# An accumulating DMA that makes the low parts of the input projection's weights in a hybrid decoder layer

## The chip, the cores and the metric

The kernel runs on one core of a Trainium2 chip. The metric is the device time of one execution in microseconds (us); lower is better. The engines are PE (TensorE: matmuls, PEld its weight loads), DVE (VectorE), ACT (ScalarE), POOL (GpSimd) and SP (SyncE, which issues most of the DMAs).

## What is computed

One decoder layer, batch 1, 1024 tokens, 1024 channels, all in float32. The part that the change touches is the product `proj = u @ w_in[l]`:

```
u = _rmsnorm(h, norm_g[l]) * (1.0 + scale) + shift
proj = u @ w_in[l]                       # [1024, 1024] x [1024, 7168]
a = conv_a * jax.nn.sigmoid(conv_bp)     # convolution branch: 31 taps, layer norm, pointwise, gate
q, k, v, ret_gate                        # retention branch: 4 heads of 256, rotary, group norm, gate
y = jnp.concatenate([y_conv, y_ret], axis=-1) @ w_out[l]
h = h + gate * y                         # then a final rms norm
```

## The kernel before

PE multiplies in a format (`F32R`) that keeps fewer bits than float32. So each operand is split into a high part (a cast to `F32R`) and a low part (the operand minus its high part), and each product is three matmuls that add up in PSUM: high by high (L71), high by low of the activations (L72), low of the weights by high (L73). This is `mm3`.

A **unit** is 128 columns of `w_in`: eight steps over the input channels, two halves of 512 tokens, three matmuls each, 48 matmuls in all. While the modulated input u is built (the head of the program), four units run along with it from weights loaded by another function. The other 44 of this kind go through `in_unit` (L246) and are counted here as units 0 to 43 in the order in which PE takes them; the eight column blocks of v are done elsewhere (`values`, L329, which calls `load_w` itself).

For each unit `load_w` (L61) does four things. SP loads the 512 KB of weights into a tile `raw` (L63). ACT casts them into `hi` (`split`, L58). DVE subtracts, `lo = raw - hi` (L59). PE then reads `hi` and `lo`. The tiles `raw`, `hi` and `lo` have two buffers each, shared with the weights of v and with those of the later projections. So the cast of unit n can only start when unit n-2 has made its last matmul on `hi`, and its matmuls on `lo` can only start when DVE is done.

The instructions of each engine run in the order that the tile framework's scheduler gives them when the kernel is built. The convolution's taps (L239, 240 instructions on DVE, in `conv_taps`) have a low priority and fill whatever time DVE has left. A unit's sums leave PSUM by ACT or DVE, at the end of the unit: by copies for the rotary embedding (L315), by sigmoid or silu activations (L254, L465, L267), or by DVE products. The retention's own matmuls are put between those of the units. POOL has little to do: a power of -0.5 for the norms (L422) and clearing the 30 columns of padding ahead of each convolution input `a` (L256), which waits until the taps have finished with that buffer, of which there are two.

After the last unit come the two halves of the output projection, the layer norm of the convolution branch and the pointwise convolution. They use `load_w` too, and the change leaves them as they are.

Of the kernel before, what the change touches and what calls it, by code (L numbers as in the profile page):

```python
# [7 lines left out]
F32 = mybir.dt.float32  # L8
F32R = mybir.dt.float32r
# [3 lines left out]
P = 128  # L13
# [3 lines left out]
KT = D // P  # L17
# [5 lines left out]
CH = 256  # L23
NCH = S // CH
HALF = 512
EARLY = (8, 0, 9, 1)  # the units that run while u is built

# columns of the packed per-channel vectors
V_C, V_SH, V_SC, V_NG, V_CB, V_LG, V_LB, V_GG, V_GB, V_CW = 0, 8, 16, 24, 32, 40, 48, 56, 64, 72
V_N = V_CW + KT * CW  # L30
# columns of the packed decay constants
K_G, K_G2, K_KD = 0, 2 * H, 4 * H
K_N = 6 * H

# [4 lines left out]
def hybrid_layer(ctx: ExitStack, tc: tile.TileContext, x, vec, c_row, ada_ss, ada_g, adab_g, w_e, w_m, w_v,  # L39
                 w_pw, w_out, final_g, cs, masks, kc, ident, out):  # L40
    nc = tc.nc
    SUB, ADD, MUL = ALU.subtract, ALU.add, ALU.mult
# [10 lines left out]
    d_yc = dram.tile([4, P, S], F32, name="d_yc")  # L53
    d_h1 = dram.tile([TT, P, D], F32, name="d_h1")

# [1 line left out]
    def split(hi, lo, src):  # L57
        nc.scalar.copy(hi, src)  # L58
        nc.vector.tensor_tensor(lo, src, hi.bitcast(F32), op=SUB)  # L59
# [1 line left out]
    def load_w(src, shape, name, pool=None):  # L61
        raw = wpool.tile(shape, F32, tag="raw", name=f"raw_{name}")
        nc.sync.dma_start(raw, src)  # L63
        pool = pool or wpool
        hi = pool.tile(shape, F32R, tag="hi", name=f"hi_{name}", bufs=2)
        lo = pool.tile(shape, F32R, tag="lo", name=f"lo_{name}", bufs=2)
        split(hi, lo, raw)
        return hi, lo

    def mm3(ps, lh, ll, rh, rl, start, stop):  # L70
        nc.tensor.matmul(ps, lh, rh, start=start, stop=False)  # L71
        nc.tensor.matmul(ps, lh, rl, start=False, stop=False)  # L72
        nc.tensor.matmul(ps, ll, rh, start=False, stop=stop)  # L73

    def unit(wh, wl, rh, rl, name, halves_first=False, pool=None, tag="mm"):
        """[128 columns of w]^T times the resident operand, both halves of its free axis."""
        ps = [(pool or mmp).tile([P, HALF], F32, tag=tag, name=f"ps_{name}_{i}") for i in range(2)]
        order = [(k, i) for k in range(KT) for i in range(2)]
        if halves_first:
            order.sort(key=lambda o: o[1])  # L80
        for k, i in order:
            sl = slice(i * HALF, (i + 1) * HALF)
            mm3(ps[i], wh[:, k], wl[:, k], rh[k][:, sl], rl[k][:, sl], k == 0, k == KT - 1)
        return ps

# [1 line left out]
    vec_t = const.tile([P, V_N], F32, name="vec_t")  # L87
    ident_t = const.tile([P, P], F32, name="ident_t")
    kc_t = const.tile([P, K_N], F32, name="kc_t")
# [10 lines left out]
        return vec_t[:, base + k:base + k + 1]  # L100

    def bcast_rsqrt(pool, psp, sums, scale, n, rb):
        """sums: [128, n] column sums (token t = 128 j + partition); rb: PSUM [128, 128 n] gets rsqrt in every row."""
        v = pool.tile([P, n], F32, tag="rs_v", name="rs_v")
        nc.vector.tensor_scalar(v, sums, scale, EPS, op0=MUL, op1=ADD)
        r = pool.tile([P, n], F32, tag="rs_r", name="rs_r")
        nc.gpsimd.tensor_tensor(r, v, mhalf[:, :n], op=ALU.pow)
        for j in range(n):
            dg = pool.tile([P, P], F32, tag="rs_d", name="rs_d", bufs=4)
            nc.vector.tensor_scalar(dg, ident_t, r[:, j:j + 1], None, op0=MUL)  # L110
            nc.tensor.matmul(rb[:, j * P:(j + 1) * P], ones_t, dg, start=True, stop=True)

# [1 line left out]
    xts = [big.tile([P, D], F32, tag="big", name=f"xt{t}", bufs=17) for t in range(TT)]  # L114
    uh = [big.tile([P, S], F32R, tag="big", name=f"uh{k}", bufs=17) for k in range(KT)]
    ul = [big.tile([P, S], F32R, tag="big", name=f"ul{k}", bufs=17) for k in range(KT)]
# [6 lines left out]
    hps = head_ctx.enter_context(tc.tile_pool(name="headps", bufs=1, space=bass.MemoryType.PSUM))  # L123

    def head():
        """Builds u tile by tile and runs the first four units along with it, k on the outside."""
        xs = hp.tile([P, KT, S], F32, name="xs")
        cbc = hp.tile([P, D], F32, name="cbc")
        junk2 = hp.tile([P, D], mybir.dt.bfloat16, name="junk2")
# [21 lines left out]
            nc.sync.dma_start(xts[t], x[t])  # L151

        def norm(t, xt_):
            """x / rms(x) of 128 tokens, turned so that features are on partitions."""
            ms = hp.tile([P, 1], F32, tag="ms", name=f"ms{t}", bufs=3)
            nc.scalar.activation(junk2, xt_, AF.Square, scale=D ** -0.5, accum_out=ms)
            nc.gpsimd.tensor_scalar(ms, ms, EPS, None, op0=ADD)
            nc.gpsimd.tensor_tensor(ms, ms, mhalf[:, 0:1], op=ALU.pow)
            nc.vector.tensor_scalar(xt_, xt_, ms, None, op0=MUL)
            for q in range(2):  # L160
                tp = hps.tile([P, 4, P], F32, tag=("paa", "pbb", "pcc", "pdd")[(2 * t + q) % 4], name=f"xp{t}{q}")
                for j in range(4):
                    k = 4 * q + j
                    nc.tensor.transpose(tp[:, j], xt_[:, k * P:(k + 1) * P], ident_t)
                dst = xs[:, 4 * q:4 * q + 4, t * P:(t + 1) * P]
                if q == 0 and t < 7:
                    nc.scalar.copy(dst, tp)
                else:
                    nc.vector.tensor_copy(dst, tp)
# [61 lines left out]
        return ps  # L231

    def conv_taps(m, ap):
        """Convolves one tile of channels; fills whatever time the vector engine has left."""
        with tc.high_priority(offset=-TAPS_LATER):
            y = convp.tile([P, S], F32, tag="y", name=f"y{m}")
            nc.vector.tensor_scalar(y, ap[:, 0:S], col(V_CW, m * CW), col(V_CB, m), op0=MUL, op1=ADD)
            for j in range(1, CW):
                nc.vector.scalar_tensor_tensor(y, ap[:, j:j + S], col(V_CW, m * CW + j), y, op0=MUL, op1=ADD)  # L239
            nc.sync.dma_start(d_y[m], y)  # L240
            if m == 0:
                nc.vector.tensor_copy(ysum, y)
            else:
                nc.vector.tensor_tensor(ysum, ysum, y, op=ADD)

    def in_unit(n):  # L246
        wh, wl = load_w(w_m[n - sum(e < n for e in EARLY)], [P, KT, P], f"w{n}")
        return unit(wh, wl, uh, ul, f"w{n}")

    def conv_pair(m, early=None):  # L250
# [25 lines left out]
    gate_steps = []  # L276

    def out_gate():
        """One step towards the residual's gate, the same in every partition."""
        k = len(gate_steps)  # L280
        if k == 0:
            gate_steps.append(const.tile([P, D], F32, name="gacc"))
        else:
            gate_steps.append(None)
        acc = gate_steps[0]
        if k < KT:
            raw = wpool.tile([P, D], F32, tag="raw", name=f"ag{k}")
            nc.sync.dma_start(raw, ada_g[k])
            if k == 0:
                nc.vector.tensor_scalar(acc, raw, cact[:, 0:1], None, op0=MUL)  # L290
            else:
                nc.vector.scalar_tensor_tensor(acc, raw, cact[:, k:k + 1], acc, op0=MUL, op1=ADD)
            return
        agb = wpool.tile([P, D], F32, tag="raw", name="agb")
        nc.sync.dma_start(agb, adab_g.broadcast_to([P, D]))
        for i in range(2):
            sl = slice(i * HALF, (i + 1) * HALF)
            gp = mmp.tile([P, HALF], F32, tag="mm", name=f"gp{i}")
            nc.tensor.matmul(gp, ones_t, acc[:, sl], start=True, stop=True)
            nc.vector.tensor_tensor(acc[:, sl], gp, agb[:, sl], op=ADD)  # L300

# [1 line left out]
    with tc.tile_pool(name="ret", bufs=1, reuse_waits="tile") as rp, \  # L303
            tc.tile_pool(name="retps", bufs=1, space=bass.MemoryType.PSUM) as rps:

# [38 lines left out]
        def retention(h, q, k, v, sg):  # L344
            state = st_h = st_l = None
            for c in range(NCH):
                ts = slice(c * CH, (c + 1) * CH)
                n = f"{h}{c}"
# [6 lines left out]

                vh, vl = chunk("vc", v[:, 2 * c:2 * c + 2])
                if c < NCH - 1:
                    # keys with tokens on partitions, decayed to the chunk's end
                    kth = rp.tile([P, 2, 2 * P], F32R, tag="kth", name=f"kth{n}")
                    ktl = rp.tile([P, 2, 2 * P], F32R, tag="ktl", name=f"ktl{n}")  # L360
                    for j in range(2):
# [8 lines left out]
                kh, kl = chunk("kc", k[:, :, ts])  # L370
                qh, ql = chunk("qc", q[:, :, ts])

                # scores, transposed: keys on partitions
                sp = rps.tile([P, 3 * P], F32, tag="sp", name=f"sp{n}")
                for d in range(2):
                    mm3(sp[:, 0:CH], kh[:, d, 0:P], kl[:, d, 0:P], qh[:, d], ql[:, d], d == 0, d == 1)
# [6 lines left out]
                sl_ = rp.tile([P, 3 * P], F32R, tag="sl", name=f"sl{n}", bufs=1)  # L383
                split(sh, sl_, sm)

                # outputs, tokens on partitions
                op = rps.tile([P, 2, 2 * P], F32, tag="op", name=f"op{n}")
                mm3(op[:, 0], sh[:, 0:P], sl_[:, 0:P], vh[:, 0], vl[:, 0], True, False)
                mm3(op[:, 1], sh[:, P:CH], sl_[:, P:CH], vh[:, 0], vl[:, 0], False, False)
# [19 lines left out]
                    st_l = rp.tile([P, 2, 2 * P], F32R, tag="stl", name=f"stl{n}")  # L409
                    split(st_h, st_l, state)  # L410

                # group norm over the head's 256 values
                st6 = rp.tile([P, 2, 6], F32, tag="st6", name=f"st6{n}", bufs=2)
                mv = rp.tile([P, 2, 2], F32, tag="mv", name=f"mv{n}", bufs=2)
                for i in range(2):
# [58 lines left out]
        f2 = ctx.enter_context(tc.tile_pool(name="fin2", bufs=1, reuse_waits="tile", side="right"))  # L474
        y3 = f2.tile([P, 3, S], F32, tag="y3", name="y3")
        negmu = f2.tile([P, S], F32, tag="y1", name="negmu")
        # layer norm, channels on partitions; what fits in before u is gone comes first
        def ln_center(m, tmp):
            if m < 3:
                yt = y3[:, m]  # L480
# [18 lines left out]
        for m in range(2, KT):  # L499
            conv_gate(m)  # L500

# [1 line left out]
    with tc.tile_pool(name="fin", bufs=1, reuse_waits="tile") as fp, \  # L503
            tc.tile_pool(name="finps", bufs=1, space=bass.MemoryType.PSUM) as fps:
        gate = gate_steps[0]
# [58 lines left out]
        fgt = fp.tile([P, D], F32, name="fgt")  # L564
        nc.sync.dma_start(fgt, final_g.broadcast_to([P, D]))

# [1 line left out]
        for m in range(KT):  # L568
            wh, wl = load_w(w_pw[m], [P, KT, P], f"pw{m}")
            ps = unit(wh, wl, zh, zl, f"pw{m}", m == KT - 1)  # L570
# [10 lines left out]
                nc.sync.dma_start(d_yc[m], cg)  # L581
            load_r(m, wpool, "raw")

# [1 line left out]
        for t in range(TT):  # L585
            hi = wpool.tile([P, KT, P], F32R, tag="hi", name=f"ych{t}")
            lo = wpool.tile([P, KT, P], F32R, tag="lo", name=f"ycl{t}")
# [46 lines left out]
def _layout(inp):  # L634
# [25 lines left out]
    ada_ss = c(ada_w[:, :2 * D].reshape(D, 2, KT, P).transpose(2, 3, 1, 0))  # L660
    ada_ss[0, :, 0] = ada_w[:, :P].reshape(KT, P, P).transpose(1, 0, 2).reshape(P, D)

    # tables that depend on the shapes alone
    f4 = np.float32
    inv = (f4(1.0) / np.power(f4(10000.0), np.linspace(0.0, 1.0, P, dtype=f4))).astype(f4)
    theta = (np.arange(S, dtype=f4)[None, :] * inv[:, None]).astype(np.float64)
# [50 lines left out]
```

## Time and profile before

| | us |
|---|---|
| median of 2 runs (1003.21 to 1003.64) | 1003.42 |
| the profiled execution, from its first to its last instruction | 1001.6 |
| of these, PE busy | 987.8 |
| DVE busy | 739.3 |
| ACT busy | 312.8 |
| POOL busy | 35.9 |

The profile is one execution on the chip. The time of a run takes in what lies around the span: the median is 1.8 us above the span of the profiled execution. The ends of matmuls are modelled, so PE's busy time is not its peak rate.

### The profile page before, as it was taken

What the parts mean: (1) busy time and instruction counts of PE and PEld (TensorE: products, weight loads), DVE (VectorE), ACT (ScalarE), POOL (GpSimd) and SP (SyncE); (2) the same over time, 40 slices, a digit from 0 to 9 for tenths busy, and PEclk for the clock granted to TensorE, in tenths of its full rate; (3) what the DMA queues carried; (4) which work ended last, traced back from release to release, by engine and by line L of the source; (5) the groups of instructions that cost most, each with busy time, mean ns of one, the idle gap of its engine ahead of it and who ended that gap; (6) DMA issues with size and microseconds to landing.
All of it is one profiled execution on the core that took longest, in us unless ns stands there. A gap on an engine that the chain in (4) does not pass through costs nothing.

```text
span 1001.6 us, 12564 instructions
## 1 busy us (share of the span) xinstructions
PE 987.8 (99%) x5108; PEld 843.6 (84%) x5108; DVE 739.3 (74%) x969; ACT 312.8 (31%) x489; POOL 35.9 (4%) x55
## 2 busy tenths in 40 slices
PE   7999999999999999999999999999999999999997
PEld 5888899888898888899888898888888888888886
DVE  6959999899998999999967679764446963442342
ACT  7831223332213322223233412443422711111221
POOL 2000000000000000100000000000000000000000
PEclk9999999999999999999999999999999999999999
DMA  9641111111132211113221022411784356541322
GB/s 351 236 168 43 43 43 64 63 64 43 64 106 74 74 63 63 43 64 127 63 84 42 25 103 63 147 64 64 264 277 152 127 172 209 187 137 63 127 95 84
DMA packets 40253, 108.80 MB, mean 109 GB/s; under 512 B 3458, under 2 KB 16002, under 8 KB 39043
## 3 DMA queue, kind: packets, MB, share of 16 engines
q1 hardware_dynamic: 40050, 107.74, 31.5%
q8 instruction: 40, 0.66, 0.3%
q10 hardware_dynamic: 144, 0.26, 0.1%
q14 instruction: 19, 0.15, 0.0%
HBM read 84.92 MB, written 23.07 MB: 108 GB/s over the span
## 4 chain that ended last, share of the span: by engine, by line
PE 96%; DVE 1%; DMA 1%; ACT 0%; issue 0%; SPq 0%; POOL 0%; POOLq 0%; DVEq 0%; ACTq 0%
PE ps_w L73 16%; PE ps_w L71 16%; PE ps_w L72 16%; PE ps_v L71 3%; PE ps_v L73 3%; PE ps_v L72 3%; PE ps_oc L73 3%; PE ps_or L72 3%; PE ps_oc L72 3%; PE ps_oc L71 3%; PE ps_or L73 3%; PE ps_pw L73 3%; PE ps_pw L71 3%; PE ps_or L71 3%; PE ps_pw L72 3%; PE op L73 1%
## 5 line engine op out<-in xcount | busy, mean ns | idle before, releaser
L239 DVE SCALAR_TENSOR_TENSOR y<-a,vec_t,y 128x1024 f32<-128x1024 f32 x240 | 300.5, 1278 | 1.3
L72 PE MATMUL ps_w<-ul,hi_w 128*128 128x512 f32 x704 | 275.2, 391 | 0.0
L73 PE MATMUL ps_w<-uh,lo_w 128*128 128x512 f32 x704 | 274.8, 391 | 0.0
L71 PE MATMUL ps_w<-uh,hi_w 128*128 128x512 f32 x704 | 274.6, 391 | 0.0
L72 PEld LDWEIGHTS ps_w<-ul,hi_w 128*128 128x128 f32 x704 | 132.3, 188 | 26.2 <-issue 0.2
L71 PEld LDWEIGHTS ps_w<-uh,hi_w 128*128 128x128 f32 x704 | 132.3, 188 | 25.9 <-issue 0.2
L73 PEld LDWEIGHTS ps_w<-uh,lo_w 128*128 128x128 f32 x704 | 132.2, 188 | 25.7
L72 PE MATMUL ps_v<-lo_v,uh 128*128 128x256 f32 x256 | 72.1, 283 | 0.0
L73 PE MATMUL ps_v<-hi_v,ul 128*128 128x256 f32 x256 | 71.8, 283 | 0.0
L71 PE MATMUL ps_v<-hi_v,uh 128*128 128x256 f32 x256 | 71.7, 283 | 0.0
L59 DVE TENSOR_TENSOR lo_w<-raw_w,hi_w 128x1024 fp32r<-128x1024 f32 x44 | 53.7, 1220 | 23.2 <-ACT hi_w L58 23.1
L58 ACT CAST hi_w<-raw_w 128x1024 fp32r<-128x1024 f32 x44 | 46.2, 1049 | 69.8 <-PE ps_w L72 27.5
L72 PE MATMUL ps_oc<-wol,ych 128*128 128x512 f32 (+1 forms) x136 | 51.2, 377 | 0.0
L73 PE MATMUL ps_oc<-woh,ycl 128*128 128x512 f32 (+1 forms) x136 | 51.2, 376 | 0.0
L71 PE MATMUL ps_oc<-woh,ych 128*128 128x512 f32 (+1 forms) x136 | 51.2, 376 | 0.0
L71 PE MATMUL ps_pw<-zh,hi_pw 128*128 128x512 f32 x128 | 49.8, 389 | 0.0
L72 PE MATMUL ps_pw<-zl,hi_pw 128*128 128x512 f32 x128 | 49.8, 389 | 0.0
L73 PE MATMUL ps_pw<-zh,lo_pw 128*128 128x512 f32 x128 | 49.8, 389 | 0.0
L72 PE MATMUL ps_or<-wol,hi_yr 128*128 128x512 f32 x128 | 49.8, 390 | 0.0
L73 PE MATMUL ps_or<-woh,lo_yr 128*128 128x512 f32 x128 | 49.6, 390 | 0.0
L71 PE MATMUL ps_or<-woh,hi_yr 128*128 128x512 f32 x128 | 49.4, 390 | 0.0
L72 PEld LDWEIGHTS ps_v<-lo_v,uh 128*128 128x128 f32 x256 | 49.0, 192 | 0.2
(219 smaller groups left out, 1552.4 us busy)
## 6 DMA issues: line engine op xcount, KB each, us to landing
raw_w<-w_m SPq DMA_DIRECT2D x44, 512.0 KB, 3.5
xt<-x SPq DMA_DIRECT2D x16, 512.0 KB, 4.5
aw<-ada_ss SPq DMA_DIRECT2D x8, 1024.0 KB, 6.7
wo<-w_out SPq DMA_DIRECT2D x16, 512.0 KB, 5.4
raw_v<-w_v SPq DMA_DIRECT2D x8, 512.0 KB, 3.5
d_y<-y SPq DMA_DIRECT2D x8, 512.0 KB, 2.9
ag<-ada_g SPq DMA_DIRECT2D x8, 512.0 KB, 3.5
d_yr<-sg SPq DMA_DIRECT2D x8, 512.0 KB, 2.8
```

The lines of the kernel that those rows point to most:

```text
L58: nc.scalar.copy(hi, src)
L59: nc.vector.tensor_tensor(lo, src, hi.bitcast(F32), op=SUB)
L71: nc.tensor.matmul(ps, lh, rh, start=start, stop=False)
L72: nc.tensor.matmul(ps, lh, rl, start=False, stop=False)
L73: nc.tensor.matmul(ps, ll, rh, start=False, stop=stop)
L239: nc.vector.scalar_tensor_tensor(y, ap[:, j:j + S], col(V_CW, m * CW + j), y, op0=MUL, op1=ADD)
```

## The change

A new function, `load_wa`, takes the place of `load_w` in `in_unit`, and nowhere else. The raw load and the cast stay. ACT then writes the negated high part into `lo` (`lo = -hi`), and a DMA issued by POOL reads the same weights from memory a second time and adds them to `lo`, which makes `raw - hi`. DVE's subtraction of these 44 units is gone. Removed comments and docstrings are left out of the diff.

```
+    def load_wa(src, shape, name):
+
+        raw = wpool.tile(shape, F32, tag="raw", name=f"raw_{name}")
+        nc.sync.dma_start(raw, src)
+        hi = wpool.tile(shape, F32R, tag="hi", name=f"hi_{name}", bufs=2)
+        lo = wpool.tile(shape, F32R, tag="lo", name=f"lo_{name}", bufs=2)
+        nc.scalar.copy(hi, raw)
+        nc.scalar.mul(lo, hi.bitcast(F32), -1.0)
+        nc.gpsimd.dma_start(lo, src, accum_op=ADD)
+        return hi, lo
...
     def in_unit(n):
-        wh, wl = load_w(w_m[n - sum(e < n for e in EARLY)], [P, KT, P], f"w{n}")
+        wh, wl = load_wa(w_m[n - sum(e < n for e in EARLY)], [P, KT, P], f"w{n}")
         return unit(wh, wl, uh, ul, f"w{n}")
```

The scheduler also orders all engines anew. In the changed kernel the cast of these units is L76, the negation L77 and the DMA L78; what stood from L70 on in the kernel before is 11 lines further down (L71 to L73 are L82 to L84).

ACT at the first three units of `in_unit`: `hi_w_717`, `hi_w_775` and `hi_w_845` before are the high parts of units 0, 1 and 2; `sig` is the sigmoid of units that ran in the head, `x_q` the copy of unit 0's sums. Before:

```order
L58 CAST hi_w_717<-raw_w_715 128x1024
L254 ACT_TABLE_LOAD
L254 ACTIVATE sig_621<-ps_e_308 128x512
L254 ACTIVATE sig_621<-ps_e_309 128x512
L254 ACTIVATE sig_662<-ps_pcc 128x512
L254 ACTIVATE sig_662<-ps_pbb 128x512
L58 CAST hi_w_777<-raw_w_775 128x1024
L315 COPY x_q_713<-ps_w_0_721 128x512
L58 CAST hi_w_847<-raw_w_845 128x1024
L315 COPY x_q_713<-ps_w_1_722 128x512
```

ACT at the same place now (`hi_w_717`, `hi_w_778`, `hi_w_849`; `lo_w` are the negated parts):

```order
L76 CAST hi_w_717<-raw_w_715 128x1024
L265 ACT_TABLE_LOAD
L265 ACTIVATE sig_621<-ps_e_308 128x512
L77 ACTIVATE lo_w_718<-hi_w_717 128x1024
L265 ACTIVATE sig_621<-ps_e_309 128x512
L265 ACTIVATE sig_662<-ps_pcc 128x512
L265 ACTIVATE sig_662<-ps_pbb 128x512
L76 CAST hi_w_778<-raw_w_776 128x1024
L77 ACTIVATE lo_w_779<-hi_w_778 128x1024
L326 COPY x_q_713<-ps_w_0_722 128x512
L76 CAST hi_w_849<-raw_w_847 128x1024
L326 COPY x_q_713<-ps_w_1_723 128x512
```

Unit 0's negation stands behind a table load and the first sigmoid, unit 1's right behind its cast, and unit 2's behind a cast and the second copy of unit 0's sums.

PE at the first matmuls of unit 16, the first after the second head's v (`hi_w_2652` and `lo_w_2653` are its parts; `kp` and `sp` are transposes and scores of the retention). Before, from the unit's third matmul on:

```order
L71 MATMUL ps_w_1_2657<-uh_93,hi_w_2652 128x512
L72 MATMUL ps_w_1_2657<-ul_101,hi_w_2652 128x512
L364 MATMUL kp_2772<-ident_t,k_2151 128x128 x2
L71 MATMUL sp_2790<-qch_2786,kch_2782 128x256
L72 MATMUL sp_2790<-qcl_2787,kch_2782 128x256
L73 MATMUL ps_w_0_2656<-uh_93,lo_w_2653 128x512
L73 MATMUL ps_w_1_2657<-uh_93,lo_w_2653 128x512
```

PE now, from the third matmul of the scores on to the unit's first matmuls on its low part (`lo_w_2669`):

```order
L84 MATMUL sp_2808<-qch_2804,kcl_2801 128x256
L82 MATMUL sp_2808<-qch_2804,kch_2800 128x256
L83 MATMUL sp_2808<-qcl_2805,kch_2800 128x256
L84 MATMUL sp_2808<-qch_2804,kcl_2801 128x256
L82 MATMUL sp_2808<-qch_2804,kch_2800 128x128
L83 MATMUL sp_2808<-qcl_2805,kch_2800 128x128
L84 MATMUL sp_2808<-qch_2804,kcl_2801 128x128
L82 MATMUL sp_2808<-qch_2804,kch_2800 128x128
L83 MATMUL sp_2808<-qcl_2805,kch_2800 128x128
L84 MATMUL sp_2808<-qch_2804,kcl_2801 128x128
L84 MATMUL ps_w_0_2673<-uh_93,lo_w_2669 128x512
L84 MATMUL ps_w_1_2674<-uh_93,lo_w_2669 128x512
```

The ten other matmuls of the scores now stand ahead of the unit's first use of `lo`. The same stands at units 26 and 35, the first after the v of heads 3 and 4.

POOL around the padding of the fifth convolution input, before (`a_2339`) and then now (`a_2354`; `lo_w_2298` is the low part of unit 14):

```order
L422 TENSOR_TENSOR rs_1647<-rs_1647,mhalf 128x2
L422 TENSOR_TENSOR rs_1758<-rs_1758,mhalf 128x2
L422 TENSOR_TENSOR rs_1839<-rs_1839,mhalf 128x2
L256 MEMSET a_2339 128x30
L256 MEMSET a_3233 128x30
```

```order
L78 DMA lo_w_2167<-w_m 128x1024
L433 TENSOR_TENSOR rs_1766<-rs_1766,mhalf 128x2
L78 DMA lo_w_2228<-w_m 128x1024
L267 MEMSET a_2354 128x30
L78 DMA lo_w_2298<-w_m 128x1024
L433 TENSOR_TENSOR rs_1847<-rs_1847,mhalf 128x2
```

The DMAs of units 12 to 14 now stand between the norms' powers and the clearing of the padding, and unit 14's stands behind that clearing. What it waits for is the last tap on the third convolution input (`a_1034` before, `a_1039` now). DVE around the instruction that follows those taps (`ysum`), before and then now:

```order
L292 SCALAR_TENSOR_TENSOR gacc<-ag_2646,cact,gacc 128x1024
L260 TENSOR_TENSOR a_2339<-ps_w_0_2347,sig_2280 128x512
L244 TENSOR_TENSOR ysum<-ysum,y_1094 128x1024
L260 TENSOR_TENSOR a_2339<-ps_w_1_2348,sig_2280 128x512
L239 SCALAR_TENSOR_TENSOR y_1982<-a_1922,vec_t,y_1982 128x1024
L59 TENSOR_TENSOR lo_v_2443<-raw_v_2440,hi_v_2442 128x1024
```

```order
L333 TENSOR_TENSOR rb_q_2146<-ps_w_0_2096,cs_t 128x512
L335 TENSOR_TENSOR rd_q_2148<-ps_w_0_2096,cs_t 128x512
L250 SCALAR_TENSOR_TENSOR y_1100<-a_1039,vec_t,y_1100 128x1024
L250 SCALAR_TENSOR_TENSOR y_1992<-a_1931,vec_t,y_1992 128x1024
L336 TENSOR_TENSOR q_2027<-q_2027,rb_q_2146 128x512
L337 TENSOR_TENSOR q_2027<-q_2027,rd_q_2148 128x512
L255 TENSOR_TENSOR ysum<-ysum,y_1100 128x1024
```

Before, the taps end beside the product that makes the fifth input (`a_2339`); now they end beside the rotary products of unit 11 (`rb_q_2146`), four units earlier.

## Rows read from the trace of the kernel before

**Rows 1.** Page of the kernel before, part 2: the span in 40 slices, tenths.
```profile
PE   7999999999999999999999999999999999999997
...
PEclk9999999999999999999999999999999999999999
```

**Rows 2.** Windows: length, busy (count) of PE, PEld, DVE, ACT, POOL; clock, DMA share, GB/s.
```profile
0.00:68.00 68.00, 60.58 (x278) 48.37 (x279) 48.99 (x75) 48.49 (x75) 7.41 (x22) 1.00 0.73 270
68.00:730.00 662.00, 662.00 (x3625) 574.33 (x3624) 560.03 (x714) 196.14 (x310) 21.91 (x22) 1.00 0.23 77
```

**Rows 3.** Groups of instructions: busy us, mean ns of one, idle before.
```profile
L59 DVE TENSOR_TENSOR lo_w<-raw_w,hi_w 128x1024 fp32r<-128x1024 f32 x44 | 53.7, 1220 | 23.2 <-ACT hi_w L58 23.1
...
L58 ACT CAST hi_w<-raw_w 128x1024 fp32r<-128x1024 f32 x44 | 46.2, 1049 | 69.8 <-PE ps_w L72 27.5 <-issue 23.7 <-PE ps_v L73 13.7
...
L237 DVE TENSOR_SCALAR y<-a,vec_t 128x1024 f32<-128x1024 f32 x8 | 6.4, 806 | 0.1
...
L489 ACT ACTIVATE sq<-yt 128x1024 f32<-128x1024 f32 x5 | 5.2, 1058 | 10.9 <-DMA d_h<-xt 7.4 <-DVE ysum L490 3.5
```

**Rows 4.** Timeline of ACT, 60 to 102 us: start, length, instruction.
```profile
62.17 1.05 ACT L58 CAST hi_w<-raw_w 128x1024 fp32r<-128x1024 f32 x1 [4.82 <-PE ps_pdd L72]
63.24 1.28 ACT L254 ACT_TABLE_LOAD   x1
64.54 1.09 ACT L254 ACTIVATE sig<-ps_e 128x512 f32<-128x512 f32 x2
...
78.52 1.05 ACT L58 CAST hi_w<-raw_w 128x1024 fp32r<-128x1024 f32 x1
79.48 0.58 ACT L315 COPY x_q<-ps_w 128x512 f32<-128x512 f32 x1
```

**Rows 5.** Timeline of PE at the first use of units 0 and 2.
```profile
68.55 0.62 PE L73 MATMUL ps_w<-uh,lo_w 128*128 128x512 f32 x2
...
89.40 0.39 PE L71 MATMUL ps_w<-uh,hi_w 128*128 128x512 f32 x1
...
89.85 0.39 PE L73 MATMUL ps_w<-uh,lo_w 128*128 128x512 f32 x1
```

**Rows 6.** Timeline of ACT, 300 to 312 us.
```profile
304.19 1.05 ACT L58 CAST hi_w<-raw_w 128x1024 fp32r<-128x1024 f32 x1 [1.27 <-PE ps_v L73]
```

**Rows 7.** Timeline of PE, 309.5 to 311.6 us.
```profile
309.75 0.40 PE L71 MATMUL ps_w<-uh,hi_w 128*128 128x512 f32 x1
...
311.13 0.63 PE L73 MATMUL ps_w<-uh,lo_w 128*128 128x512 f32 x2
```

**Rows 8.** Timeline of ACT, 150 to 162 us.
```profile
152.20 1.05 ACT L58 CAST hi_w<-raw_w 128x1024 fp32r<-128x1024 f32 x1 [3.81 <-PE ps_v L73]
```

**Rows 9.** Timeline of PE, 160 to 161 us.
```profile
160.63 0.39 PE L73 MATMUL ps_w<-uh,lo_w 128*128 128x512 f32 x1
```

**Rows 10.** Timeline of ACT, 705 to 712 us.
```profile
708.22 1.04 ACT L58 CAST hi_w<-raw_w 128x1024 fp32r<-128x1024 f32 x1
```

**Rows 11.** Timeline of PE, 718.9 to 719.8 us.
```profile
719.49 0.39 PE L73 MATMUL ps_w<-uh,lo_w 128*128 128x512 f32 x1
```

**Rows 12.** DMA issues: KB each, median us from issue to landing.
```profile
raw_w<-w_m SPq DMA_DIRECT2D x44, 512.0 KB, 3.5
...
aw<-ada_ss SPq DMA_DIRECT2D x8, 1024.0 KB, 6.7
...
d_y<-y SPq DMA_DIRECT2D x8, 512.0 KB, 2.9
```

**Rows 13.** Timeline of POOL, 50 to 530 us.
```profile
283.29 0.12 POOL L256 MEMSET a<- 128x30 f32 x1 [29.38 <-DVE y L239]
...
409.19 2.67 POOL L422 TENSOR_TENSOR rs<-rs,mhalf 128x2 f32<-128x2 f32 x1 [25.56 <-DVE rs L421]
...
520.94 0.69 POOL L422 TENSOR_TENSOR rs<-rs,mhalf 128x2 f32<-128x2 f32 x1 [13.18 <-DVE rs L421]
```

**Rows 14.** Timeline of PE, 264.2 to 265.2 us.
```profile
264.91 0.39 PE L73 MATMUL ps_w<-uh,lo_w 128*128 128x512 f32 x1
```

## Prediction

> **What bounds the kernel now.** I read the slices first: PE is at 9 tenths from the second slice to the last but one, with its clock at 9 throughout [rows 1]. The windows view sharpens it: from 68 to 730 us, the stretch that holds all 44 units of `in_unit`, PE is busy for 662.00 of 662.00 us, while DVE is busy for 560, ACT for 196, POOL for 22, and the DMA engines for 0.23 of the time [rows 2]. PE's clock is at its upper level (2.4 GHz) there. So no engine but PE sets the end of this stretch, and work taken from DVE gives PE nothing back. What can change the time is a unit whose parts come later than PE wants them. That is read from the groups of instructions (what a cast waits for) and from the timelines of ACT and PE.
>
> **What goes.** 44 subtractions of 1220 ns [rows 3], 53.7 us of DVE. They lie beside PE's matmuls, so their going is worth nothing in time. DVE's other work, the taps above all, comes earlier by it.
>
> **What comes, per unit.** The negation on ACT is bounded by the cast of the same shape (1049 ns) and by an activation of it (1058) [rows 3]; I take 1.06 us. 44 of them are 47 us on an engine busy for 196 of 662, so ACT doesn't become the bound, but the negation is a step in a chain: cast, negation, DMA, first matmul on `lo`. The cast starts when the unit two before lets its buffer go; its idle time is put down to PE [rows 3]. What the chain may take from the end of the negation to the landing I call a unit's allowance: its first L73 matmul in the trace, less its cast's start, less the cast, less what ACT now does between (from its order), less the negation.
>
> - Unit 2: the cast starts at 78.52, a copy of 0.58 follows [rows 4], the first L73 is at 89.85 [rows 5]. 11.33 - 1.05 - 0.6 - 1.06 = 8.6 us.
> - Unit 43, the last: 719.49 - 708.22 = 11.27 [rows 10, 11]. The 0.6 us evacuation stays between cast and negation; its first L73 now has two more matmuls ahead of it (0.45 us, the distance of 89.40 to 89.85 for two [rows 5]): 9.0.
> - Unit 0: the cast starts at 62.17, then a table load, then a sigmoid that starts at 64.54 and takes half of 1.09 (alone some 0.6), and only then the negation, which ends at 66.2 [rows 4]. First L73: 68.55 [rows 5]. 2.4 us.
> - Unit 6: 160.63 - 152.20 = 8.43 [rows 8, 9]; less 2.11 is 6.3.
> - Unit 16: 311.13 - 304.19 = 6.94 [rows 6, 7]; less 2.11 is 4.8. But ten more score matmuls now stand ahead of its first L73. From 309.75 to 311.13 PE did four matmuls of 512 columns, at 0.23 each (0.45 for two [rows 5]), and four small ones, so 0.115 for a small one: 1.1 us more, 5.9. Units 26 and 35 stand at the same place of heads 3 and 4 and count the same.
>
> The same subtraction over all 44 gives 7.9 to 9.3 for fifteen units and more than 9.4 for the other 24.
>
> **The unknown: the accumulating DMA.** The trace has none, nor any DMA issued by POOL. Counted from the end of the negation to the landing, it is bounded so. Below: a 512 KB load lands 3.5 us after its issue [rows 12]; the new one can't be quicker, since it moves those bytes too and reads `lo` besides. Above: a 1024 KB load (6.7), a 512 KB store after it (2.9) [rows 12] and the slowest small instruction of POOL for making the transfer (2.67) [rows 13]: 12.3. I take the 1024 KB load, which reads as many bytes, and a POOL instruction at its quickest (0.69): 7.4 us. Row 6.7 is nearest because two streams of 512 KB are read; the writes go out while the reads come in. The load of `raw` for the unit after next now starts at the end of the cast, so the two transfers overlap; I have no row for that and leave it in the range.
>
> The Trainium skill (DMA: Bandwidth & Descriptors, section Anatomy of one DMA — SWDGE (gpsimd) path) gives a POOL-issued DMA 2.0 us and its bytes at 436 GB/s. For two reads of 512 KB that is an estimate of 4.4 us, and the sum by it would be 2.0 us, 1005.4. No run here shows an accumulating one yet.
>
> **The sum.** A unit whose landing is later than its allowance stops PE for the difference. That delays later units' need and the release of buffers alike; so with two buffers a steady lateness costs its excess once in two units. At 7.4: unit 0 5.0, unit 6 1.1, units 16, 26 and 35 1.5 each: 10.6 us. The rest have at least 0.5 in hand. The profiled execution spans 1001.6; 1012.2 with this. The median of the runs lies 1.8 above the span (1003.42), so I predict 1014.0. The extra 23 MB of reads find DMA engines that are busy for 0.23 of the stretch [rows 2]. POOL's queue is the other path: the power (L422) and the clearing of padding are now among the DMAs, in order.
>
> **The rivals.**
>
> *It is hidden.* At 3.5 us only unit 0 is late, by 1.1; at 5.9, by 3.5. Time: 1004.5 to 1007. For it: DMA engines are mostly idle. Against it: two reads where the row has one, and the load of `raw` beside them.
>
> *Two buffers are too few (slower).* In the plain stretches a unit is 48 matmuls at 0.227 us, 10.9 us, and its partner in the other buffer as long; once cast, negation and landing exceed what that leaves, PE waits at every second unit. It decides from a DMA of about 8.6 us on: the bookkeeping gives 20 us at 8.9, 47 at 11 and 71 at 12.3 (33 of it at the five short units, the rest over some 17 others). Time at 8.9: 1024; at 11: 1051; at 12.3: 1074. For it: every row under the 7.4 is an idle plain transfer. Against it: it needs the three terms end to end.
>
> *POOL is slow while DVE runs (slower).* The same power takes 2.67 us at 409, when the taps run, and 0.69 at 521 [rows 13]. If making the transfer suffers alike, the DMA takes 2.0 more, 9.4: the sum is 26 us, 1029. The Trainium skill (SBUF — State Buffer, section Who interferes with whom) says that a POOL-issued DMA is starved while DVE is in a two-port mode, and that a DVE instruction with two SBUF inputs only holds up POOL's reads. By that the power's rows would be reads held up, and making a transfer would be safe but for DVE instructions such as the eight of 806 ns [rows 3].
>
> *POOL's queue (slower).* Unit 14's DMA stands behind clearing the fifth padding, which was done at 283.29 [rows 13]; PE wants that unit at 264.91 [rows 14]. Were the taps no earlier, PE would stop for 283.3 + 7.4 - 264.9 = 26 us: 1040. Against it: fourteen subtractions less (17 us), and DVE's new order, which ends those taps beside unit 11's products. Units 12 and 13 lie between, 22 us for a DMA of 7.4.
>
> *Faster.* PE is idle for 13.8 us of the span (the table), 7.4 of them before 68 us [rows 2]; only these could be had, and no instruction there changes but unit 0's.
>
> **How the numbers follow.** My forecast (5.9 to 8.9 us for the DMA) has a chance of 0.38, its own range 1007 to 1023. Hidden: 0.24. Two buffers: 0.25. POOL slowed by DVE: 0.08. POOL's queue: 0.04. Faster: 0.01. A run here can tell about 2%, 20 us, from no change. Faster by more than that: 0.01. Within it, the forecast and the hidden case: 0.62. Slower, the other three: 0.37. The range goes from 1004 (below it 3 in 100) to 1055, a DMA of about 11.4 us, above which I put 1 in 10.
>
> **What would show it.** Right: DMAs by POOL that land 6 to 9 us after the negation, a gap on PE before unit 0's first L84 of some 5 us, gaps of 1 to 2 at units 6, 16, 26 and 35, none elsewhere, DVE busy for 54 us less, ACT for 47 more. Wrong: gaps at every second unit of the plain stretches (two buffers), landings that shorten after 500 us, when the taps thin out (POOL slowed), a DMA whose idle time ends with DVE's taps (queue), or gaps on PE in the retention that no weight explains, which I have counted at nothing.

## The result, and the profile after

| | before | after |
|---|---|---|
| median of the first runs, us | 1003.42 (2 runs) | 1012.38 (2 runs, 1012.06 to 1012.70) |
| ratio, 95% interval | | 1.0091 [1.0061, 1.0120] |
| timed again | 1003.60 (11 runs) | 1013.43 (4 runs, 1012.46 to 1014.00) |
| ratio, 95% interval | | 1.0097 [1.0083, 1.0111] |
| span of the profiled execution | 1001.6 | 1010.3 |

The change costs 9 to 10 us, 0.9 to 1.0%. The profile after is the execution of 1012.06 us. Its page gives the engines' busy time, PE's slices, the clock, and the DMA issues with their median time to landing; the slices answer to [rows 1], the raw load to [rows 12]:

```profile
PE 989.8 (98%) x5108; PEld 844.6 (84%) x5108; DVE 696.3 (69%) x925; ACT 356.8 (35%) x533; POOL 69.4 (7%) x99
...
PE   7989999999999999999999999999999999999996
...
PEclk9999999999999999999999999999999999999999
...
raw_w<-w_m SPq DMA_DIRECT2D x44, 512.0 KB, 3.5
lo_w<-w_m POOLq DMA_DIRECT2D x44, 512.0 KB, 5.9
```

The new DMA lands 5.9 us after its issue, the raw load still after 3.5. PE's busy time hardly moved (987.8 before), so the loss is mostly idle time. The windows that answer to [rows 2] (busy us of PE, PEld, DVE, ACT, POOL; clock, DMA share, GB/s) show it:

```profile
0.00:68.00 68.00, 60.74 (x276) 48.91 (x277) 46.61 (x73) 48.31 (x74) 9.16 (x23) 0.97 0.74 270
68.00:730.00 662.00, 656.39 (x3595) 568.87 (x3594) 511.45 (x666) 235.51 (x351) 53.61 (x65) 1.00 0.42 106
```

From 68 to 730 us PE is now busy for 656.39 of 662.00: it stands still for 5.6 us where it had no gap. DVE's load there fell from 560.03 to 511.45 and ACT's rose from 196.14 to 235.51. PE waited for neither of them in this stretch, in either kernel. The groups that answer to [rows 3] (busy us, mean ns; the first line is that of before):

```profile
L239 DVE SCALAR_TENSOR_TENSOR y<-a,vec_t,y 128x1024 f32<-128x1024 f32 x240 | 300.5, 1278 | 1.3
...
L250 DVE SCALAR_TENSOR_TENSOR y<-a,vec_t,y 128x1024 f32<-128x1024 f32 x240 | 303.5, 1281 | 3.0
...
L77 ACT ACTIVATE lo_w<-hi_w 128x1024 fp32r<-128x1024 f32 x44 | 46.8, 1063 | 0.5
L76 ACT CAST hi_w<-raw_w 128x1024 fp32r<-128x1024 f32 x44 | 46.1, 1049 | 64.7 <-PE ps_w L83 41.5 <-PE ps_v L84 18.4 <-PE ps_pdd L83 4.8
L78 POOL DMA_DIRECT2D lo_w<-w_m x44 | 38.8, 882 | 489.7 <-ACT lo_w L77 489.7
```

The negation costs 1063 ns, and POOL spends 882 ns on making each transfer. PE's timeline, in five short windows, shows where it stops (start, length, the idle time ahead in brackets and what ended it):

```profile
68.79 0.39 PE L83 MATMUL ps_w<-ul,hi_w 128*128 128x512 f32 x1
72.74 0.73 PE L84 MATMUL ps_w<-uh,lo_w 128*128 128x512 f32 x2 [3.56 <-DMA lo_w<-w_m]
...
165.10 0.50 PE L84 MATMUL ps_w<-uh,lo_w 128*128 128x512 f32 x1
...
317.25 0.72 PE L84 MATMUL ps_w<-uh,lo_w 128*128 128x512 f32 x2 [0.28 <-DMA lo_w<-w_m]
...
471.99 0.49 PE L84 MATMUL ps_w<-uh,lo_w 128*128 128x512 f32 x1 [0.77 <-DMA lo_w<-w_m]
...
616.15 0.73 PE L84 MATMUL ps_w<-uh,lo_w 128*128 128x512 f32 x2 [0.99 <-DMA lo_w<-w_m]
```

The stops stand before the first use of `lo` of units 0, 16, 26 and 35: 3.56, 0.28, 0.77 and 0.99 us, all ended by the new DMA. Unit 6 (165.10) has no idle time in brackets; its matmul starts 0.16 us late by the pitch of its neighbours. There is no other stop after 31 us. ACT and POOL at unit 0 show the chain behind the first of them. ACT, answering to [rows 4]:

```profile
62.64 1.05 ACT L76 CAST hi_w<-raw_w 128x1024 fp32r<-128x1024 f32 x1 [4.82 <-PE ps_pdd L83]
63.72 1.28 ACT L265 ACT_TABLE_LOAD   x1
65.01 0.60 ACT L265 ACTIVATE sig<-ps_e 128x512 f32<-128x512 f32 x1
65.50 1.05 ACT L77 ACTIVATE lo_w<-hi_w 128x1024 fp32r<-128x1024 f32 x1
```

POOL at unit 0, at the padding of the fifth convolution input [rows 13], and at two powers:

```profile
66.88 1.06 POOL L78 DMA_DIRECT2D lo_w<-w_m  x1 [47.87 <-ACT lo_w L77]
...
247.31 0.46 POOL L267 MEMSET a<- 128x30 f32 x1
260.96 0.86 POOL L78 DMA_DIRECT2D lo_w<-w_m  x1 [13.20 <-ACT lo_w L77]
264.78 1.73 POOL L433 TENSOR_TENSOR rs<-rs,mhalf 128x2 f32<-128x2 f32 x1 [2.96 <-DVE rs L432]
...
510.83 0.90 POOL L78 DMA_DIRECT2D lo_w<-w_m  x1 [7.03 <-ACT lo_w L77]
515.00 0.71 POOL L433 TENSOR_TENSOR rs<-rs,mhalf 128x2 f32<-128x2 f32 x1 [3.27 <-DVE rs L432]
```

The negation of unit 0 ends at 66.56, POOL starts at 66.88, PE goes on at 72.74: 6.2 us from the end of the negation to the use. The DMA of unit 14 (260.96) did not wait for the padding, which was cleared at 247.31, where it had been 283.29 before.

**Where the 8.7 us between the two profiled spans are.** PE's idle time (span less busy) rose from 13.8 to 20.5 us, by 6.7: the four stops are 5.6 of it, the head and the tail 1.1. PE's busy time rose by 2.0. Another cut is by place: the first matmul of unit 0 (`ps_w`) and the first of the output projection, which follows unit 43 (`ps_or`), before and then now.

```profile
67.64 0.39 PE L71 MATMUL ps_w<-uh,hi_w 128*128 128x512 f32 x1
...
729.92 0.39 PE L71 MATMUL ps_or<-woh,hi_yr 128*128 128x512 f32 x1
```

```profile
68.11 0.39 PE L82 MATMUL ps_w<-uh,hi_w 128*128 128x512 f32 x1
...
737.09 0.39 PE L82 MATMUL ps_or<-woh,hi_yr 128*128 128x512 f32 x1
```

The head is 0.5 us longer; its clock was lower in this execution (0.97 over the first 68 us against 1.00 before [rows 2]). The stretch of the units is 6.7 us longer: the stops' 5.6, and 1.1 in matmuls that come further apart, as at unit 6 and behind the stops. What follows the units is 1.5 us longer, though the change leaves it as it is.

### The profile page after: what moved, and what is told of

Same layout as the page of the kernel before. It is cut to its first block, busy times and chain, and to the rows that moved or that the text cites. A ratio compares the mean times of both kernels' runs of the same rounds, so it can differ in the third digit from the quotient of the medians.

```text
span 1010.3 us, 12637 instructions
## 1 busy us (share of the span) xinstructions
PE 989.8 (98%) x5108; PEld 844.6 (84%) x5108; DVE 696.3 (69%) x925; ACT 356.8 (35%) x533; POOL 69.4 (7%) x99
## 4 chain that ended last, share of the span: by engine, by line
PE 94%; DMA 2%; issue 2%; ACT 1%; DVE 0%; POOL 0%; POOLq 0%; DVEq 0%; ACTq 0%
PE ps_w L84 16%; PE ps_w L83 16%; PE ps_w L82 16%; PE ps_or L84 3%; PE ps_oc L83 3%; PE ps_oc L82 3%; PE ps_oc L84 3%; PE ps_or L83 3%; PE ps_pw L84 3%; PE ps_pw L83 3%; PE ps_or L82 3%; PE ps_pw L82 3%; PE ps_v L82 3%; PE ps_v L83 3%; PE ps_v L84 3%; DMA lo_w<-w_m 2%
## 5 line engine op out<-in xcount | busy, mean ns | idle before, releaser
L250 DVE SCALAR_TENSOR_TENSOR y<-a,vec_t,y 128x1024 f32<-128x1024 f32 x240 | 303.5, 1281 | 3.0
L84 PE MATMUL ps_w<-uh,lo_w 128*128 128x512 f32 x704 | 274.8, 392 | 5.6 <-DMA lo_w<-w_m 5.6
L82 PE MATMUL ps_w<-uh,hi_w 128*128 128x512 f32 x704 | 275.3, 391 | 0.0
L84 PEld LDWEIGHTS ps_w<-uh,lo_w 128*128 128x128 f32 x704 | 132.0, 188 | 32.6 <-DMA lo_w<-w_m 6.9
L82 PEld LDWEIGHTS ps_w<-uh,hi_w 128*128 128x128 f32 x704 | 132.3, 188 | 26.4 <-issue 0.2
L78 POOL DMA_DIRECT2D lo_w<-w_m x44 | 38.8, 882 | 489.7 <-ACT lo_w L77 489.7
L84 PE MATMUL ps_v<-hi_v,ul 128*128 128x256 f32 x256 | 72.0, 283 | 0.0
L82 PE MATMUL ps_v<-hi_v,uh 128*128 128x256 f32 x256 | 71.9, 283 | 0.0
L76 ACT CAST hi_w<-raw_w 128x1024 fp32r<-128x1024 f32 x44 | 46.1, 1049 | 64.7 <-PE ps_w L83 41.5
L84 PE MATMUL ps_oc<-woh,ycl 128*128 128x512 f32 (+1 forms) x136 | 51.2, 376 | 0.0
L82 PE MATMUL ps_oc<-woh,ych 128*128 128x512 f32 (+1 forms) x136 | 51.2, 376 | 0.0
L82 PE MATMUL ps_pw<-zh,hi_pw 128*128 128x512 f32 x128 | 49.8, 389 | 0.0
L84 PE MATMUL ps_pw<-zh,lo_pw 128*128 128x512 f32 x128 | 49.8, 389 | 0.0
L84 PE MATMUL ps_or<-woh,lo_yr 128*128 128x512 f32 x128 | 49.6, 391 | 0.0
L82 PE MATMUL ps_or<-woh,hi_yr 128*128 128x512 f32 x128 | 49.3, 390 | 0.0
```

What stands on the lines that cost most here:

```text
L76: nc.scalar.copy(hi, raw)
L78: nc.gpsimd.dma_start(lo, src, accum_op=ADD)
```

## Experiments

Theory A: the loss is those stops of PE, at the few units whose parts PE wants soonest. The rivals put it on the traffic, on ACT's negations, or on the scheduler's new order, spread over all units. All are edits of the changed kernel, timed in alternation with the kernel before.

| kernel | median, us | before | ratio, 95% interval |
|---|---|---|---|
| e1: five units old | 1004.23 | 1003.23 | 1.0013 [1.0004, 1.0022] |
| e2: five units only | 1015.11 | 1003.23 | 1.0123 [1.0109, 1.0137] |
| e3: ACT negates, DVE adds | 1004.96 | 1003.23 | 1.0017 [1.0008, 1.0025] |
| e4: two DMAs in a row | 1084.44 | 1003.23 | 1.0802 [1.0785, 1.0819] |
| e5: the changed kernel again | 1013.43 | 1003.60 | 1.0097 [1.0083, 1.0111] |
| e6: unit 0 old | 1007.53 | 1003.60 | 1.0047 [1.0033, 1.0061] |
| e7: DMA without the addition | 1006.38 | 1003.60 | 1.0028 [1.0017, 1.0039] |
| e8: DMA in two halves | 1008.60 | 1003.60 | 1.0053 [1.0041, 1.0066] |
| e9: unit 0 negated on DVE | 1010.69 | 1003.44 | 1.0074 [1.0060, 1.0088] |
| e10: e8 and e9 together | 1006.97 | 1003.44 | 1.0034 [1.0021, 1.0047] |

### e1 and e2: which units pay

Units 0, 6, 16, 26 and 35 are the columns 24, 40, 42, 44 and 46.

```
     def in_unit(n):
-        wh, wl = load_wa(...)
+        load = load_w if n in (24, 40, 42, 44, 46) else load_wa    # e1; e2 has the two exchanged
+        wh, wl = load(...)
```

> The five units with the shortest allowance (0, 6, 16, 26, 35) get the old load with DVE's subtraction back; the other 39 keep the accumulating DMA. Theory A (the 9.0 us are the stops of PE at units 0, 16, 26 and 35, 5.6 us in the trace of after, their edges, and little else; a DMA of about 6.1 us from the end of the negation is hidden at every other unit): 1003.5 to 1006, no gap on PE after 31 us. Rival B (the 23 MB of extra reads, POOL's issues and the new order of the engines cost a little at every unit): 39 of 44 shares of 9.0 us remain, 1011.4. Rival C (ACT's 47 us of negations are what costs): the same 1011.

> The reverse: only units 0, 6, 16, 26 and 35 make their low parts by the accumulating DMA, the other 39 by DVE's subtraction. Theory A: nearly all of the loss, 1009 to 1012.5, with the same stops on PE (about 3.6 us at unit 0, 0.3 to 1.2 at units 16, 26 and 35). Rivals B and C: 5 of 44 shares of 9.0 us, 1004.4.

With the five units put back, 1.0 us of the loss is left, and PE's timeline has no stop after 31 us. What is left doesn't lie at the units: in e1's profile, whose span is 1.4 us over that of before, unit 0's first matmul starts at 67.94 and the output projection's at 730.12, so the head is 0.3 us longer, the units take 662.2 us (662.3 before), and 1.2 us lie behind them. With the five alone, all of the loss is there and more: 11.9 us, so that 1015.11 is 2.6 us over theory A's range. The rivals' 1011.4 and 1004.4 are both out by 7 us or more. The other 39 units make their low parts by the DMA for nothing that this can see: the traffic, ACT's negations and POOL's issues are hidden.

Why e2 loses more than the whole change did in e5 (11.9 us against 9.8), its profile shows: the stops sum to 7.2 us there (5.7 in e5's), and PE's clock falls twice (once in e5). Windows of 1 us at the end of unit 0's stop (the last three numbers: clock, DMA share, GB/s):

```profile
71.00:72.00 1.00, 0.00 (x0) 0.00 (x0) 1.00 (x2) 0.00 (x0) 0.00 (x0) 1.00 0.35 66
72.00:73.00 1.00, 0.70 (x2) 0.61 (x3) 1.00 (x2) 0.00 (x0) 0.00 (x0) 0.59 0.00 0
73.00:74.00 1.00, 1.00 (x4) 0.81 (x3) 1.00 (x3) 0.00 (x0) 0.00 (x0) 0.50 0.00 0
...
76.00:77.00 1.00, 1.00 (x6) 0.83 (x5) 1.00 (x2) 0.00 (x0) 0.00 (x0) 1.00 0.01 4
```

PE's timeline at the same place and at unit 26, and the window there:

```profile
72.30 1.22 PE L84 MATMUL ps_w<-uh,lo_w 128*128 128x512 f32 x2 [3.52 <-DMA lo_w<-w_m]
73.32 0.63 PE L82 MATMUL ps_w<-uh,hi_w 128*128 128x512 f32 x1
73.74 0.63 PE L83 MATMUL ps_w<-ul,hi_w 128*128 128x512 f32 x1
...
475.52 0.80 PE L84 MATMUL ps_w<-uh,lo_w 128*128 128x512 f32 x1 [2.56 <-DMA lo_w<-w_m]
```

```profile
470.00:480.00 10.00, 7.44 (x37) 6.20 (x36) 9.60 (x11) 5.23 (x8) 0.00 (x0) 0.83 0.61 175
```

When PE goes on at 72.30 after 3.52 us, its clock is at the lower level, 1.2 GHz (0.50), for some 3 us: matmuls come every 0.43 us in place of 0.23. Unit 26 waits 2.56 us in this execution, and the clock falls there too (0.83 from 470 to 480 us). PE's busy time is 4.1 us over that of before, 3.4 of it by these two falls (0.17 of 10 us each). Unit 26's DMA landed 8.6 us after the negation; two other transfers of 512 KB, issued by SP at 465.83 and 466.22, ran beside it (its own issue was at 467.20). That they made it late was not tested.

### e3: ACT alone

```
-        nc.gpsimd.dma_start(lo, src, accum_op=ADD)
+        nc.vector.tensor_tensor(lo, raw, lo.bitcast(F32), op=ADD)
```

> ACT's negation stays at all 44 units, but DVE adds the raw weights to it in place (lo = lo + raw), so no DMA is issued by POOL and DVE has its 44 instructions back. Theory A: from the end of the negation to the low part 1.2 us, at most 2.5 behind a tap of 1.28 us: below every allowance but perhaps unit 0's 2.6, so 1003.4 to 1005. Rival B: the new order stays but the traffic goes, 1003.4 to 1007. Rival C (ACT): 1011 to 1012.4.

1.7 us [0.8, 2.5] are left without the DMA. Rival C falls: ACT's 44 negations are not what costs 9 us. 1004.96 lies in the ranges of theory A and rival B alike, so e3 doesn't tell these two apart; e1 and e2 do. PE's small stops there (0.33 us before an L82 of the projection, 0.62 in the output projection) wait for ACT and DVE and not for a low part.

### e4: a DMA twice as long

```
-        nc.scalar.mul(lo, hi.bitcast(F32), -1.0)
+        nc.scalar.mul(lo, hi.bitcast(F32), -2.0)
         nc.gpsimd.dma_start(lo, src, accum_op=ADD)
+        nc.gpsimd.dma_start(lo, src, accum_op=ADD)
```

> The accumulating DMA is issued twice, the second adding to what the first left; the negation is by -2, so that the low part comes out twice too large. From the end of the negation to the second landing: 0.3 + 5.9 + 0.3 + 5.9, some 12.4 us. Bookkeeping with two buffers (a steady lateness counts once in two units), at 12.3 us: 71 us over the kernel before, 1074 (1070 to 1085), with stops at about 20 units. Rival D (only the short units stop, the others have slack that the bookkeeping does not see): 9.9 + 6.0 + 3 x 6.4 = 35 us, 1039. Rival E (each unit pays its whole lateness, since nothing is regained from one unit to the next): some 109 us, 1112.

1084.44: the rivals D (1039) and E (1112) fall, and the bookkeeping is the nearest, at the upper end of its range. The busy times on its page:

```profile
PE 1015.5 (93%) x5108; PEld 858.0 (79%) x5108; DVE 696.9 (64%) x925; ACT 355.1 (33%) x533; POOL 105.3 (10%) x143
```

and its waits (us in all, times, the longest):

```profile
POOL lo_w L79 <- DMA lo_w<-w_m: 239.2, 41, 8.8
...
PE ps_w L85 <- DMA lo_w<-w_m: 54.5, 19, 7.6
```

PE stops 19 times for 54.5 us, and its own work takes 27.7 us more than before (1015.5 against 987.8), with the clock at a mean of 0.972 over the execution and at 0.69 from 70 to 80 us, behind the first long stop. The second landing comes 12.7 us (median) after the negation, up to 18.4, because POOL stands still while the second DMA waits for the first, and the next unit's first one stands behind it. With each unit's own measured landing the bookkeeping gives some 75 to 80 us, all of it stops. Measured are 54.5 of stops, and 82 with the longer work. So its sum is near, but not its kind of loss: it has no clock in it, and whether the longer work took the place of stops was not tested. At 12.7 us two buffers are too few; where that sets in (8.6 by the prediction) no run tried.

### e5 and e6: unit 0 by itself

e6 calls `load_w` for column 24 alone.

> The changed kernel as it is, timed beside the three that follow. Its two runs were 1012.06 and 1012.70. If its stop at unit 0 (3.56 us) leaves PE at the upper clock, as in its profile, 1011.5 to 1013; if the clock falls after that stop in some executions, as it did after the 3.52 us stop of the kernel with five accumulating units alone, up to 1.7 us more in those.

> Only unit 0 gets the old load back. Theory A (stops add up): 3.56 us and its edge less, 1008 to 1009, with stops of 0.3 to 1.2 us left at units 16, 26 and 35. Rival F (a stop given back at unit 0 comes back later, since the later units were helped by the shift): 1010.5 or more, with longer stops at units 2, 6 or 16.

e6 is 5.9 us faster than e5, and its 1007.53 lies 0.5 us under theory A's range, which had no clock in it. The stop at unit 0 in e5's profile is 3.54 us; the windows behind it show the rest:

```profile
70.00:80.00 10.00, 8.10 (x29) 6.51 (x30) 10.00 (x10) 0.15 (x1) 0.88 (x1) 0.83 0.55 124
80.00:90.00 10.00, 10.00 (x46) 8.28 (x45) 6.62 (x7) 2.98 (x4) 0.87 (x1) 1.00 0.37 84
```

A clock of 0.83 over 10 us is 1.7 us lost. In the first profile the stop of 3.56 us at the same place left the clock at 1.00, and the clock had fallen in the head instead (0.83 from 20 to 30 us). So the same stop costs some 3.6 or 5.2 us from one execution to the next, as the expectation had it; the 0.7 us that e6 gains beyond that are not placed. Rival F falls: the stops left at units 16, 26 and 35 are 0.50, 0.91 and 0.37 us, no longer than before.

### e7 and e8: what the DMA's time is made of

```
-        nc.gpsimd.dma_start(lo, src, accum_op=ADD)
+        nc.gpsimd.dma_start(lo, src)                                            # e7
+        for i in range(2):                                                      # e8
+            nc.gpsimd.dma_start(lo[:, 4 * i:4 * i + 4], src[:, 4 * i:4 * i + 4], accum_op=ADD)
```

> The same DMA by POOL without the addition: it overwrites the low part with the whole weights, so the subtraction is left out. The order of all engines is that of the changed kernel. Theory G (the second read, of the low part, makes the transfer 5.9 us long): a plain copy lands 0.87 us of POOL's own time plus the 3.5 us of SP's load after its issue, 4.4 us; from the end of the negation 4.7; unit 0 stops PE for 2.1 us, the others not at all: 1006 to 1007.5. Rival H (POOL's issue and the way of its descriptors make it long, the addition is free): 5.5 to 5.9 us to the landing, the same four stops, 1011 to 1012.5.

> The accumulating DMA is issued as two of 256 KB, one for the first four input-channel blocks and one for the last four; PE's first matmul on the low part waits for the first alone. Theory J (part of the 5.9 us goes with the bytes, as with 0.87 us issue + 2 us + bytes): the first half lands 4.4 to 4.9 us after its issue; unit 0's stop 2.2 to 2.7 us, none or 0.2 at units 16, 26, 35: 1006.5 to 1008.5. Rival K (the time is fixed per DMA, or POOL's second issue delays the first's transfer): the first half lands at 5.5 us or later, 1011 to 1013, and 44 more issues of 0.87 us on POOL that nobody waits for.

The low parts' own view in e7, whose engines keep the order of the changed kernel (ns min/median/max of POOL's issue, and the landing), and then in e8, where it takes both halves together:

```profile
L78 POOL DMA_DIRECT2D lo_w<-w_m x44: 527/537/782, 66.2 to 712.8; - x44
...
DMA to landing us min/median/max: 3.7/4.5/7.9
```

```profile
L79 POOL DMA_DIRECT2D lo_w<-w_m x88: 862/1136/1463, 66.0 to 713.9; - x88
...
DMA to landing us min/median/max: 3.9/5.3/10.1
```

PE's first use of `lo`, in e7 and then in e8:

```profile
70.12 0.50 PE L84 MATMUL ps_w<-uh,lo_w 128*128 128x512 f32 x1 [1.60 <-DMA lo_w<-w_m]
```

```profile
70.28 0.70 PE L85 MATMUL ps_w<-uh,lo_w 128*128 128x512 f32 x2 [2.02 <-DMA lo_w<-w_m]
```

Theory G holds: a plain copy lands after 4.5 us (POOL's 0.54 and the 3.5 of SP's load would make 4.0), and only unit 0 stops, for 1.60 us. The addition makes POOL's issue 0.33 us longer (0.865 against 0.537) and the rest of the way about 1 us. In e8 the first half lands 4.3 us (median) after its issue, the second 5.6 after its own: halving the bytes takes 1.6 us off what PE waits for, though the second half then lands 6.5 us after the negation where the whole did at 6.2. Unit 0 stops for 2.02 us, unit 16 for 0.57 (0.2 at most were expected). Theory J holds in kind; the time, 1008.60, is 0.1 us over its range. Rival H and rival K fall.

### e9 and e10: the place of unit 0's negation

```
+        if name == "w24":
+            nc.vector.tensor_scalar(lo, hi.bitcast(F32), -1.0, None, op0=MUL)
+        else:
+            nc.scalar.mul(lo, hi.bitcast(F32), -1.0)
```

> Unit 0's negation alone is moved from ACT, where it stands behind a table load and a sigmoid, to DVE, which is idle when the cast ends; the accumulating DMA of all units stays. The negation then ends at about 64.5 to 65 us in place of 66.6. Theory A (the stop is the chain's length minus the allowance, and the place in ACT's order is 1.5 to 2 us of it): unit 0's stop 1.6 to 2.0 us in place of 3.5, no lower clock after it, 1009.5 to 1011.5. Rival L (the DMA is limited by something else at that time, the weights' other transfers): the stop stays over 3 us, 1012.5 to 1014.

> The same with the DMA issued in two halves. Theory A: unit 0's stop, 2.02 us with the halves alone, shrinks by the same 1.5 to 2 us to 0.5 or less; 1005 to 1007, within a few us of the kernel before, with all 44 low parts still made by the DMA. It is not expected to be faster than the kernel before, whose PE has no gap after 31 us. Rival L: 1008.5.

DVE's timeline in e9, then PE's at the first use of `lo` in e9 and in e10:

```profile
63.40 0.69 DVE L78 TENSOR_SCALAR lo_w<-hi_w 128x1024 fp32r<-128x1024 f32 x1 [5.18 <-ACT hi_w L76]
```

```profile
70.66 0.73 PE L87 MATMUL ps_w<-uh,lo_w 128*128 128x512 f32 x2 [1.82 <-DMA lo_w<-w_m]
```

```profile
69.45 0.47 PE L88 MATMUL ps_w<-uh,lo_w 128*128 128x512 f32 x1 [0.50 <-DMA lo_w<-w_m]
```

The negation ends at 64.09 in place of 66.56, and the stop shrinks from 3.56 to 1.82 us, in e10 to 0.50. Unit 0's stop is thus the chain's length less the allowance, and 1.7 us of it came from making the negation on ACT: mostly the place in ACT's order, but the instruction is also 0.36 us shorter on DVE (0.69 against 1.05), which the run doesn't separate. Rival L falls. In e9 the clock fell behind the 1.82 us as well (0.83 from 70 to 80 us), against the expectation. e10 keeps all 44 low parts on the DMA and is 3.5 us over the kernel before. No version here is faster than before: after 31 us that kernel's PE has no gap to fill. A third buffer for `hi` and `lo`, which would start the casts earlier, wasn't tried.

## Why the prediction came out right

**What bounds the kernel.** Right. DVE's 43.0 us less (739.3 to 696.3) gave nothing, and PE lost what the late low parts cost. The prediction said 54 us less, the sum of 44 subtractions. The page's busy time counts a moment once in which the records of two instructions overlap: 240 taps of 1278 ns make 306.7 us, and their line has 300.5. The other work didn't take longer: a tap took 1278 ns before and takes 1281 now. ACT's 44.0 us more (312.8 to 356.8; said: 47) are short in the same way.

**The allowances.** Right within 0.3 us at the units that the prediction works out. In the profile after, the time from the negation to PE's use, less the stop, is 6.2 - 3.56 = 2.6 us at unit 0 (said: 2.4), and 6.1 at units 16, 26 and 35 (6.34 - 0.28, 6.82 - 0.77, 7.05 - 0.99; said: 5.9). Of the other 39, eleven have 8.4 to 9.3 us and the rest over 9.7 (said: fifteen from 7.9 to 9.3, the rest over 9.4). e1 and e2 show that no unit but these and unit 6 pays.

**The DMA.** This is the term that was mis-sized: "I take the 1024 KB load, which reads as many bytes, and a POOL instruction at its quickest (0.69): 7.4 us". It is 6.2 us (median, 5.6 to 8.9). e7 puts the addition at 1.4 us, about 1 of it in the transfer, where the rows for 512 and 1024 KB [rows 12] differ by 3.2. The larger of these rows was a poor model: its eight loads run in the head, where the DMA engines were busy for 0.73 of the time, against 0.23 in the stretch of the units [rows 2]. So it wasn't the idle transfer that the prediction, in its rival of two buffers, takes every row to be. The bookkeeping, with each unit's measured landing put in, gives 6.2 us for the stops (3.7, 0.1, 0.4, 0.9, 1.1), and 5.6 were measured: the rule was sound and its input too high.

**The sum.** 10.6 us predicted, 9.0 to 9.8 measured, but not of the same parts: 5.6 of stops, and some 3 to 4 that I had at nothing. Of these the lower clock is up to 1.7 (e5, e6), and what e1 leaves when no stop is left is 1.0 [0.4, 2.2]. The latter lies in the head and behind the units, by e1's profile; e3 has as much without any DMA, and why is open. The stops were put 5 us too high and these parts 3 to 4 too low, and that the two nearly cancel is luck: the time came out nearer than its terms deserve.

**The rivals.** *Hidden*: the DMA is hidden at 39 units, and late at units 0, 16, 26 and 35, and by 0.16 us at unit 6; e7, at 4.8 us from the negation to the landing (median), is that case: its stop is at unit 0 alone, and its 1006.38 lies in the 1004.5 to 1007 given. *Two buffers*: not so at 6.2 us; e4, at 12.7, is that case. *POOL slowed by DVE*: not so. POOL's issue took 0.86 to 0.90 us at nearly all units (at most 1.06, at unit 0), while a power was at 1.73 us at 264.78 and 0.71 at 515.00. By the landings it would be wrong too (us min/median/max of the units before and behind 500 us):

```profile
DMA to landing us min/median/max: 5.4/5.8/7.6
...
DMA to landing us min/median/max: 5.3/6.6/8.6
```

They grow longer where the taps thin out. The trace agrees here with the rule of the Trainium skill (SBUF — State Buffer, Who interferes with whom) that a DVE instruction with two SBUF inputs, such as a tap, holds up POOL's reads of SBUF but not its writes. The exception that the prediction names shows twice: where POOL's issue for unit 11 met one of the eight DVE instructions of 806 ns, it took 1.05 us in e9 and 1.21 in e1, though 0.90 in the changed kernel, where that instruction had begun first. *POOL's queue*: not so, the padding was cleared 13.7 us ahead of unit 14's DMA. *The skill's price* (DMA: Bandwidth & Descriptors, Anatomy of one DMA — SWDGE (gpsimd) path): the 4.4 us worked out from it as an estimate is too low for the accumulating DMA, which took 5.9 from its issue; for the plain 512 KB copy the page's formula gives an estimate of 3.2 us, and e7 measured 4.5. The measurement decides.

## What to carry to other kernels

Work moved off an engine that doesn't bound the kernel gives nothing, and a longer chain costs only at the places where the consumer wants its result soonest: here five of 44 tiles held nearly the whole loss, each the first after another phase of the program (the head, or a head's v). So list for each tile the time between its producer's start and its first use, and keep the slower way of making it for those with room. The accumulating DMA of 512 KB was hidden here wherever 8.4 us or more lay between the data it adds to and the first use, and late where 6.1 did; issuing it in two pieces that are consumed in order shortened the wait for the first (e8).

## What was not expected of the hardware

- The clock after a stop. PE's clock fell to its lower level at stops of 1.82 (e9), 2.56 and 3.52 (e2) and 3.54 us (e5), and stayed at the upper one after 1.60 (e7), 2.02 (e8) and 3.56 us (the first profile of the changed kernel). By the granted clock (0.83 over 10 us) each fall cost 1.7 us. So a stop has a price that its own length doesn't tell, and that changes from one execution to the next. The clock also fell in the head (0.83 from 20 to 30 us) in the profiles of the changed kernel, e1, e3, e6 and e10, two of which have no late low part at all.
- The addition in this DMA is cheap: 1.4 us on 4.5 at 512 KB, of which 0.33 are POOL's own.
- The time to landing rose late in the stretch, from a median of 5.8 us before 500 us to 6.6 behind. Other transfers run there as well (DMA share 0.49 from 600 to 730 us, 0.36 from 500 to 600); which of them it waits for wasn't tried.
